# Preparing Strassen steps in an interleaved order, and 210 instead of 188 of them

## The chip, the core and the metric

The kernel runs on one NeuronCore of a Trainium2 chip. Times are device microseconds of that core. The weights are read from HBM in every run.

## What is computed

A decoder block for 256 tokens of 4096 channels in float32. Cut to what matters here:

```python
h = rmsnorm(x, norm_w)
proj = einsum('bsd,de->bse', h, w_in)            # 4096 x 20480
u_p, z_p, u_c, b_c, c_c, z_c, g_logit = split(proj)
y_pool = causal_multiscale_pool(u_p, pool_w, pool_scale) * silu(z_p)
y_conv = b_c * conv_b_w3(c_c * u_c) * silu(z_c)  # causal depthwise width 3
br = einsum('bsnc,ncd->bsnd', stack([y_pool, y_conv]), w_branch)   # 2 x 2048 x 4096
merged = sum(sigmoid(g_logit + gate_b) * br)
out = rmsnorm(x + einsum('bsd,de->bse', merged, w_out), final_norm_w)
```

Almost all of the arithmetic is in three products with large weights: `w_in`, `w_branch` and `w_out`.

## The kernel before

**Units and steps.** The work is cut into 32 units, each of which makes 256 tokens by 1024 output columns: twenty for `w_in` (named cu, cc, cz, cb for the convolution branch, pz, pu for the pooling branch, g for the gates, each with an index), eight for `w_branch` (b0_0 to b1_3) and four for `w_out` (o0 to o3). A unit of `w_in` or `w_out` has 16 steps, a unit of `w_branch` 8, so there are 448 steps on large weights. A step takes one 1 MB piece of weights (256 rows by 1024 columns), which SyncE loads into one of the `raw` buffers, and multiplies it with the 256 channels of activations that stand in `arena`.

**Precision.** Float32 is reached by splitting: ScalarE copies a value to the rounded type float32r (the high part, `act`), VectorE subtracts the high part from the value (the low part, `sub`). Each product is three matmuls: high by high, high by low, low by high. Split weights lie in `ring`, a circular store counted in blocks of 128 x 256 values; space is freed as TensorE's matmuls use it up.

**Two kinds of step.** A plain step ("P") has 8 products of 128 x 128 by 128 x 512, that is 24 matmuls; it splits its weights in two halves of 1024 columns per partition, one `act` and one `sub` each. A Strassen step ("S", the Winograd form) has 7 products, 21 matmuls, but adds weights before it splits them. Its VectorE instructions are, in this order: `V` (two sums at once, 1024 wide), the first half of `raw` overwritten with a sum (512), the low part of the three unsummed blocks (1536), another sum in `raw` (512), the low part of `V` (1024), the low part of the two sums in `raw` (1024). Ring space for it comes in pieces of 12, 8 and 8; a P step takes twice 8.

**Which steps are S.** For each unit a sequence of P and S is written out or spread by a formula. An operand in `arena` must be stored with its Strassen sums to serve an S step: 7 of the 16 channel pairs are stored so (`NS_X`), and 9 as P (`NP_X`). One of the P pairs, called `LATE`, has its sums computed and split separately and kept in other buffers (`late_sums`, `late_split`, `early_place`, `late_m`, the DRAM tile `late_d`), so that up to 8 steps of a unit can be S.

**The order of the work.** All instructions are emitted by one Python program that walks through the matmuls in TensorE's order; each engine then executes its own instructions in the order in which they were emitted. After each group of matmuls `after_group` calls `tick`, which takes one item from `queue` (the unit's epilogue, with `gap(n)` as pauses) and one piece of filling the next operands into `arena` (`pop_fill`), and then `pump`. `pump` emits the next pieces of preparation (`micros`) of the steps to come, up to `AHEAD` = 3 steps ahead, as far as the ring has room by then; it also issues the load into a `raw` buffer whose previous step is prepared. At the end of a unit the four shared banks with Strassen products are combined by `joins`, and the other banks are copied by ScalarE and added by `combine`.

VectorE's instructions of the preparation are all at line L72 (`tt`, through `add` and `sub`), ScalarE's at L69 (`act`), the matmuls of the steps at L1283 (`multiply`), loads by SyncE at L87, transfers by GpSimd at L91 and L94.

Of the kernel before, what the change touches and what calls it, by code (L numbers as in the profile page):

```python
# [26 lines left out]
F32 = mybir.dt.float32  # L27
# [5 lines left out]
P = 128  # L33
# [9 lines left out]
NP_X, NS_X = 9, 7  # L43
NB = 1
NP_Y, NS_Y = (6, 5), (2, 3)
RING = 60
NRAW = 3
# [9 lines left out]
def hybrid_block(ctx: ExitStack, tc: tile.TileContext, x, x_t, norm_t, w_first, w_in, pool_w, pool_scale,  # L57
# [70 lines left out]
    late_d = dram.tile([P, 5, P], F32, name="late_d")  # L128
# [62 lines left out]
    class Operand:  # L191


        def __init__(self, kind, view, region):
            self.kind, self.view, self.region = kind, view, region
            self.ready = False
            self.more = None
            self.more_ready = False

        def block(self, part, i):  # L200

            if self.kind == "S":
                return self.view[:, part, i]
            if i in self.more:
                return self.more[i][:, part]
            return self.view[:, part, {A12: 0, A22: 0, A11: 1, A21: 1}[i], i in (A22, A21)]
# [32 lines left out]

    rg = Ring(RING)  # L240

# [5 lines left out]
    class Step:  # L247
# [7 lines left out]
        def micros(self):  # L255
# [27 lines left out]
            if self.kind == "P":  # L283
                self.blocks, self.h, self.l = [None] * 2, [None] * 2, [None] * 2
                return self.pre + [(8, None, half(0)), (8, None, half(1))] + self.post
            if self.kind == "S":
                q = r.rearrange("p (i n) -> p i n", i=4)
                tv = V

                def sums(_):  # L290
                    add(tv, q[:, 0:1].to_broadcast([P, 2, NH]), q[:, 1:3])

                def direct(block):
                    self.bd = block
                    d = piece(block, 0, 12).rearrange("p (i a n) -> p i a n", i=3, a=2)
                    self.dh, self.dl = d[:, :, 0], d[:, :, 1]
                    act(self.dh, q[:, 1:4])
# [11 lines left out]
                def t24(block):  # L309
                    self.b24 = block  # L310
                    t = piece(block, 0, 8).rearrange("p (i a n) -> p i a n", i=2, a=2)
                    self.h24, self.l24 = t[:, :, 0], t[:, :, 1]
                    act(self.h24, q[:, 0:2])
                    sub(self.l24, q[:, 0:2], self.h24.bitcast(F32))

                return self.pre + self.post + [(0, None, sums), (12, None, direct), (8, None, t13), (8, None, t24)]
            if self.kind == "B":
                def parts(block):
# [4 lines left out]
                    sub(self.l, R, self.h.bitcast(F32))  # L323

                return [(16, lambda: self.unit.flags.get("base"), parts)]
            if self.kind == "M":
# [4 lines left out]
                def weights(block):  # L331
# [5 lines left out]
                    sub(self.l, q, self.h.bitcast(F32))  # L337

# [265 lines left out]
    LAST_FIRST = ('cc0',)  # L604
    SPREAD = {"cc1":(8,1),"cb1":(8,2),"cu1":{4,5,7,9,10,12,13,15},"cb0":(8,2),"cz0":(7,5),"pz0":{5,7,8,10,11,13,15},"pu0":(7,),"cz1":(7,5),"g1_3":(6,0),"pz1":(7,),"g0_0":(7,),"pu1":{4,6,8,10,12,13,15},"cc0":{2,4,6,8,10,13,15}}
# [26 lines left out]
    def in_unit(name, col, epi, seq=None, **kw):  # L632
        def src(i):
            return win[col // NU, i]
        if name in SPREAD:
            at = SPREAD[name]
            seq = at_places(at) if isinstance(at, set) else spread_sequence(*at)
# [5 lines left out]
        units.append(Unit(name, src, seq or seq_late, x_ops, epi, scaled=True, **kw))  # L643
# [3 lines left out]
    def conv_units(c, first=False):  # L647
# [32 lines left out]
        in_unit(f"cu{c}", base, lambda u: [], seq=seq_0 if first else spread_sequence(NS_X, 4), dst=Y)  # L680
        in_unit(f"cc{c}", base + 2 * HALF, c_epi, seq=seq_even if c else None)
        in_unit(f"cz{c}", base + 3 * HALF, z_epi)
        in_unit(f"cb{c}", base + HALF, b_epi, seq=seq_even)


    def pool_units(c):
# [5 lines left out]
        in_unit(f"pz{c}", HALF + c * NU, z_epi, seq=None if c else seq_turned)  # L692
# [4 lines left out]
    def make_bands(c):  # L697
        nonlocal sa, Y
        if c == 0:
            x_ops[LATE].more_ready = False  # L700

# [78 lines left out]
    def gate_unit(n, c, before=None):  # L780
# [7 lines left out]
        seq = {(0, 0): seq_late, (1, 3): spread_sequence(few)}.get((n, c), seq_even)  # L788
        if (n, c) in ((0,1),(1,1),(0,2),(1,2),(0,3),(1,0),):
            seq = spread_sequence(NS_X + 1, 1 if c else 2)  # L790
# [27 lines left out]

    def out_unit(c):
# [14 lines left out]
        seq = seq_even if c else seq_late  # L834
        if c in (2,):
            seq = spread_sequence(NS_X + 1)
        if c == 1:
            seq = at_places({2,4,6,7,9,11,13,15})

            late_s = [i for k, i in seq if k == 'S']  # L840
            late_s = iter(late_s[1:] + late_s[:1])
            seq = [(k, next(late_s) if k == 'S' else i) for k, i in seq]
        if c == 3:

            seq = spread_sequence(NS_X, 1, TAIL + 0)
        if c == 2:
            seq = at_places({2,4,6,7,9,11,13,15})
# [133 lines left out]
    def insert(u, c, owner):  # L981
# [6 lines left out]
        rest = psteps[5:]  # L988
        while ssteps:
            seq.append(ssteps.pop(0))  # L990
            if rest:
                seq.append(rest.pop(0))
        seq += rest
# [132 lines left out]
    LATE = NP_X - 1  # L1126

    def late_sums():
        o = x_ops[LATE]
        h, l = (o.view[:, part].bitcast(F32) for part in range(2))  # L1130
        q = sa[:, 4:8].rearrange("p (k t) c -> p k t c", t=2)
        add(q, h, l)
        q = q.rearrange("p k t c -> p k (t c)")
        mul(q, q, rbc[:, None].to_broadcast([P, 2, T]))
        sums_s(sa, [sa[:, i] for i in range(4, 8)])
        mul(sa[:, Q3], sa[:, Q3], std)
        move(late_d[:, 0:4], sa[:, 0:4])
        move(late_d[:, 4], sa[:, A11])

    def late_place(pool, o, blocks):  # L1140
        n = len(blocks)
        q = pool.tile([P, 2, n, P], F32R, name="sums")
        o.more = {b: q[:, :, i] for i, b in enumerate(blocks)}
        return q

    def late_split(o, place, src):

        q = []
        return [lambda: (q.append(place()), act(q[0][:, 0], src)),
                lambda: (sub(q[0][:, 1], src, q[0][:, 0].bitcast(F32)), setattr(o, "more_ready", True))]  # L1150

    early = []

    def early_place():

        pool = replace_by("early")
        src = pool.tile([P, 5, P], F32, name="early_src")
        move(src, late_d)
        early.extend(late_split(x_ops[LATE], lambda: late_place(pool, x_ops[LATE], (Q3, Q5, Q6, Q7, A11)), src))

    late = []

    def late_m():
        nonlocal Y
        pool = replace_by("late_m", lower)
        stages.pop()
        Y = pool.tile([P, 1, NU], F32, name="Y")
        sums_s(sa, [sa[:, i] for i in range(4, 8)])
        late.append(late_place(pool, m_ops[LATE], (Q3, Q5, Q6, Q7)))

# [12 lines left out]
    seconds = {14: 10, 15: 11, 16: 12, 17: 13, 19: 14, 21: 15, 28: 9}  # L1183
# [15 lines left out]
    before(23, late_sums)  # L1199
    before(40, early_place)  # L1200
    before(41, lambda: early[0]())
    before(42, lambda: early[1]())
# [30 lines left out]

    def pump():

        while True:
# [10 lines left out]
            if i < len(steps) and i <= state["limit"]:  # L1247
                s = steps[i]
                if s.src is None or s.raw is not None:
                    if state["micros"] is None:  # L1250
                        state["micros"] = deque(s.micros())
                    if state["micros"]:
                        size, guard, fn = state["micros"][0]
# [14 lines left out]
    for s in steps:  # L1268
        s.prepared = False
# [305 lines left out]
```

## Time and profile before

| | |
|---|---|
| median of three runs | 2378.24 us (2378.23 to 2379.2) |
| span of the profiled execution, first to last instruction | 2376.6 us |
| TensorE busy | 2364.3 us (99%), 10540 matmuls |
| VectorE busy | 2170.1 us (91%), 2195 instructions |
| ScalarE busy | 1392.8 us (59%) |
| GpSimd busy | 86.0 us (4%) |
| DMA | 551.25 MB, mean 232 GB/s |
| granted clock of TensorE | 0.999 |

The profile names a group of instructions by its line, engine and operation, then what it writes and reads (`ring<-raw`), the shape and the count; then busy time, mean duration, and the time that the engine idled before them with what ended the wait. The profile gives the profiled execution by its span only; the median of the runs is 1.6 us above that span.

### The profile page before, as it was taken

The numbers are of one execution on the slowest core, as the hardware profiler recorded it, in microseconds if no ns is written. First come the engines' busy times: TensorE is split into PE (matmuls) and PEld (weight loads), VectorE is DVE, ScalarE is ACT, GpSimd is POOL, SyncE is SP. The second block draws the span as 40 slices with busy tenths as digits, with TensorE's granted clock in tenths as the row PEclk, the third lists the DMA queues.
The fourth block names the chain that finished last, engine by engine and source line by source line (L and its number), as shares of the span: only waits on it lengthen the run. The fifth ranks groups of instructions, "written<-read, shape, count | busy, mean of one in ns | idle before, by whom it ended". The sixth has DMA issues, their size and how long they took to land.

```text
span 2376.6 us, 27878 instructions
## 1 busy us (share of the span) xinstructions
PE 2364.3 (99%) x10540; PEld 1957.5 (82%) x10540; DVE 2170.1 (91%) x2195; ACT 1392.8 (59%) x1452; POOL 86.0 (4%) x153
## 2 busy tenths in 40 slices
PE   9999999999999999999999999999999999999998
PEld 7888888888888888888888888888888888888886
DVE  8999999989989978979999999999898898799998
ACT  7565665656546555556655656556664556566554
POOL 0000000000010010000000000000100001000000
PEclk9999999999999999999999999999999999999999
DMA  8464665655665646655776667667766667567666
GB/s 337 161 238 170 235 251 211 217 211 213 212 239 217 238 183 221 231 200 201 259 247 214 235 237 235 228 238 260 263 249 230 226 250 289 209 214 265 241 240 264
DMA packets 83559, 551.25 MB, mean 232 GB/s; under 512 B 9616, under 2 KB 9872, under 8 KB 22240
## 3 DMA queue, kind: packets, MB, share of 16 engines
q1 hardware_dynamic: 68800, 484.51, 54.7%
q0 software_dynamic: 14192, 63.90, 9.6%
q8 instruction: 82, 1.34, 0.2%
q10 hardware_dynamic: 432, 1.07, 0.1%
q14 instruction: 53, 0.43, 0.1%
HBM read 516.60 MB, written 25.49 MB: 228 GB/s over the span
## 4 chain that ended last, share of the span: by engine, by line
PE 98%; DVE 1%; DMA 1%; ACT 0%; SPq 0%; issue 0%; DVEq 0%; ACTq 0%
PE sums L1283 74%; PE shared L1283 21%; PE shared L766 1%; PE shared L509 1%; DMA raw<-in_w_in_dram 0%; DVE R L72 0%; DVE ring L72 0%; DMA raw<-in_w_out_dram 0%; ACT ring L69 0%; PE shared L745 0%; SPq L87 0%; PE shared L746 0%; PE shared L748 0%; SPq L162 0%; ACT V L69 0%
## 5 line engine op out<-in xcount | busy, mean ns | idle before, releaser
L1283 PE MATMUL sums<-ring,arena 128*128 128x512 f32 x7890 | 1858.2, 390 | 0.5 <-ACT arena L69 0.4
L1283 PEld LDWEIGHTS sums<-ring,arena 128*128 128x128 f32 x7890 | 1478.3, 188 | 307.8 <-ACT ring L69 1.2
L69 ACT ACTIVATE ring<-raw 128x1024 fp32r<-128x1024 f32 (+2 forms) x902 | 997.5, 1145 | 703.9 <-DVE raw L72 297.3
L72 DVE TENSOR_TENSOR ring<-raw,ring 128x1024 fp32r<-128x1024 f32 (+2 forms) x902 | 1176.5, 1335 | 142.5 <-ACT ring L69 108.6
L1283 PE MATMUL shared<-ring,arena 128*128 128x512 f32 x2118 | 535.2, 389 | 0.0
L1283 PEld LDWEIGHTS shared<-ring,arena 128*128 128x128 f32 x2118 | 397.6, 188 | 82.5
L69 ACT ACTIVATE ring<-V 128x1024 fp32r<-128x1024 f32 x188 | 198.8, 1058 | 148.3 <-DVE V L72 112.7
L72 DVE TENSOR_TENSOR V<-raw 128x1024 f32<-128x1024 f32 x188 | 229.3, 1220 | 4.7 <-DMA raw<-in_w_in_dram 2.6
L72 DVE TENSOR_TENSOR ring<-V,ring 128x1024 fp32r<-128x1024 f32 x188 | 229.3, 1220 | 0.5 <-ACT ring L69 0.5
L72 DVE TENSOR_TENSOR raw<-raw 128x512 f32<-128x512 f32 x188 | 130.2, 693 | 6.5
L72 DVE TENSOR_TENSOR raw<-V,raw 128x512 f32<-128x512 f32 x188 | 130.0, 692 | 5.8
L72 DVE TENSOR_TENSOR R<-R,E 128x1024 f32<-128x1024 f32 (+1 forms) x49 | 77.5, 1591 | 1.6 <-ACT E L69 0.9
L72 DVE TENSOR_TENSOR R<-R,shared 128x512 f32<-128x512 f32 x87 | 59.5, 684 | 8.9 <-ACT R L69 5.0
L69 ACT ACTIVATE E<-sums,rin 128x512 f32<-128x512 f32 x76 | 50.0, 685 | 15.7 <-PE sums L1283 15.7
L69 ACT ACTIVATE arena<-sa 128x512 fp32r<-128x512 f32 (+2 forms) x42 | 22.4, 559 | 35.5 <-DVE sa L72 35.5
L1283 PE MATMUL shared<-ring,sums 128*128 128x512 f32 x138 | 35.9, 396 | 0.0
L1283 PEld LDWEIGHTS shared<-ring,sums 128*128 128x128 f32 x138 | 25.9, 188 | 6.0
L94 POOL DMA_DIRECT2D R<-E x8 | 7.2, 980 | 513.6 <-ACT ring L69 337.9
L69 ACT ACTIVATE E<-sums 128x512 f32<-128x512 f32 x40 | 22.2, 592 | 5.4 <-PE sums L1283 5.1
L72 DVE TENSOR_TENSOR arena<-sa,arena 128x512 fp32r<-128x512 f32 (+2 forms) x42 | 24.4, 606 | 0.7 <-ACT arena L69 0.7
L94 POOL DMA_DIRECT2D R<-in_gate_b_dram x9 | 10.1, 1119 | 356.0 <-DVE R L72 348.3
L509 PEld LDWEIGHTS shared<-ident,R 128*128 128x128 f32 x160 | 19.4, 140 | 4.2
(149 smaller groups left out, 515.8 us busy)
## 6 DMA issues: line engine op xcount, KB each, us to landing
raw<-in_w_in_dram SPq DMA_DIRECT2D x318, 1024.0 KB, 4.9
raw<-in_w_branch_dram SPq DMA_DIRECT2D x64, 1024.0 KB, 5.4
raw<-in_w_out_dram SPq DMA_DIRECT2D x64, 1024.0 KB, 5.0
gates_d<-R POOLq DMA_DIRECT2D x8, 1024.0 KB, 9.1
R<-in_gate_b_dram POOLq DMA_DIRECT2D x7, 1024.0 KB, 11.2
R<-E POOLq DMA_DIRECT2D x4, 1024.0 KB, 8.7
raw<-in_pool_w_dram SPq DMA_DIRECT2D x4, 1024.0 KB, 5.0
Y<-gates_d POOLq DMA_DIRECT2D x4, 1024.0 KB, 7.9
```

The lines of the kernel that those rows point to most:

```text
L69: return pin(nc.scalar.activation(dst, src, func, **kw))
L72: return pin(nc.vector.tensor_tensor(out=dst, in0=a, in1=b, op=op))
L94: return pin(nc.gpsimd.dma_start(dst, src, accum_op=ALU.add))
L509: pin(nc.tensor.transpose(shared(j)[:, i * T + t * P:i * T + (t + 1) * P], src[:, t, c:c + P], ident))
L766: pin(nc.tensor.matmul(o, a[:, k, ts], b[:, k], start=(k, i) == (0, 0), stop=(k, i) == (3, 2)))
L1283: pin(nc.tensor.matmul(ps, lhs, rhs, start=n == 0, stop=n == u.total[b] - 1))
```

## The change

- `NP_X, NS_X` goes from 9, 7 to 7, 9: nine channel pairs are stored with Strassen sums, two more than before, and the special `LATE` pair with all its code goes. `NB` (how many S slots of `arena` are two blocks longer) goes from 1 to 2, `RING` from 60 to 58 blocks, `NRAW` from 3 to 4 buffers. The space that software DMAs keep for descriptors is set to 2048 bytes of each partition.
- The P and S places of every unit are written out (`PLACES`, `GATE`, `OUT`). 210 of the 448 steps are S, before 188.
- The preparation of an S step is reordered and interleaved with its neighbours. ScalarE's copy of the three unsummed blocks comes first; then VectorE makes `V`, then the low part that the S step before still owes (`settle`), then the low part of the three blocks, then the first sum in `raw`; then the split of `V`, then the second sum. The low part of the two sums is put on `held` and emitted inside the next step's preparation. `head_of_next` emits the first ScalarE copy of the next step ahead of the last copy of this one. A P step's halves are split into a `high` and a `low` piece each.

The core of the diff:

```diff
-NP_X, NS_X = 9, 7
-NB = 1
+NP_X, NS_X = 7, 9
+NB = 2
-RING = 60
-NRAW = 3
+RING = 58
+NRAW = 4
...
+    held = []
+
+    def settle():
+
+        while held:
+            held.pop(0)()
...
+                def low(n):
+                    def f(_):
+                        sub(self.l[n], q[:, :, n * NH:(n + 1) * NH], self.h[n].bitcast(F32))
+                        settle()
+                    return f
+                return self.pre + [(8, None, high(0)), (0, None, low(0)), (8, None, high(1)), (0, None, low(1))] + self.post
...
-                def sums(_):
-                    add(tv, q[:, 0:1].to_broadcast([P, 2, NH]), q[:, 1:3])
                 def direct(block):
...
                     act(self.dh, q[:, 1:4])
+                def sums(_):
+                    add(tv, q[:, 0:1].to_broadcast([P, 2, NH]), q[:, 1:3])
+                    settle()
+                    sub(self.dl, q[:, 1:4], self.dh.bitcast(F32))
                     add(q[:, 0], tv[:, 0], q[:, 2])
-                    sub(self.dl, q[:, 1:4], self.dh.bitcast(F32))
-                    add(q[:, 1], q[:, 0], q[:, 3])
...
+                def t24(_):
+                    add(q[:, 1], q[:, 0], q[:, 3])
                     act(self.h24, q[:, 0:2])
-                    sub(self.l24, q[:, 0:2], self.h24.bitcast(F32))
-                return self.pre + self.post + [(0, None, sums), (12, None, direct), (8, None, t13), (8, None, t24)]
+                    def low24():
+                        sub(self.l24, q[:, 0:2], self.h24.bitcast(F32))
+                        self.prepared = True
+                    held.append(low24)
+                return self.pre + self.post + [(12, None, direct), (0, None, sums), (8, None, t13), (8, None, place24),
+                                               (0, lambda: head_of_next(self), t24)]
...
+        "cb0": (3, 5, 6, 8, 9, 11, 12, 14, 15),
...
+    GATE = (2, 4, 5, 7, 8, 10, 11, 13, 15)
...
+    OUT = ((5, 7, 8, 10, 11, 13, 15), (2, 4, 6, 7, 9, 11, 12, 13, 15), (2, 4, 6, 7, 9, 11, 13, 15),
+           (1, 3, 4, 6, 7, 9, 10, 12))
...
-    seconds = {14: 10, 15: 11, 16: 12, 17: 13, 19: 14, 21: 15, 28: 9}
+    seconds = {14: 10, 15: 11, 16: 12, 17: 13, 19: 14, 21: 15, 28: 9, 32: 8, 36: 7}
...
+    def head_of_next(s):
+
+        i = state["np"] + 1
+        if i == len(steps):
+            return True
+        t = steps[i]
+        if t.kind not in "PS" or t.pre or t.post and t.kind == "S" or t.started:
+            return True
+        if i <= state["limit"] and t.raw is not None:
+            t.started = micro(t)
+        return t.started or state["np"] <= state["now"] + 1
...
-    nc = _bacc.Bacc("TRN2", target_bir_lowering=False, num_devices=1)
+    nc = _bacc.Bacc("TRN2", target_bir_lowering=False, num_devices=1,
+                     dynamic_dma_scratch_size=2048)
```

More of the change, by code (lines that the diff above doesn't have):

```diff
@@ L1123, in x_parts @@
             sub(o.view[:, 1, a:b], sa[:, a:b], o.view[:, 0, a:b].bitcast(F32))
[L1126 to L1169, printed above, removed]
     def before(i, fn, *args):
@@ L1375, in hybrid_block @@
         for st in u.steps:
+            if not st.prepared:
+                settle()
             assert st.prepared, (u.name, st.kind)
@@ L1422, in hybrid_block @@
     for st in lead:
+        if not st.prepared:
+            settle()
         assert st.prepared, (last.name, st.kind)
```

120 lines of the change are left out of this document (51 added, 69 removed), and 12 rows, old and new, of the table PLACES.

## The prediction

> **What bounds the kernel now.** I read the page first, then the waits of every engine, then the timelines of TensorE and VectorE, then one unit alone.
>
> ```profile
> span 2376.6 us, 27878 instructions
> ...
> PE 2364.3 (99%) x10540; PEld 1957.5 (82%) x10540; DVE 2170.1 (91%) x2195; ACT 1392.8 (59%) x1452; POOL 86.0 (4%) x153
> ...
> PE 98%; DVE 1%; DMA 1%; ACT 0%; SPq 0%; issue 0%; DVEq 0%; ACTq 0%
> ```
>
> TensorE holds 98% of the chain that ended last. A busy TensorE can still be a stalled one, so the waits decide; these are all that the trace has for TensorE and its weight loads:
>
> ```profile
> PE shared L1034 <- DVE rout L1039: 1.1, 1, 1.1
> PE sums L1283 <- ACT arena L69: 0.4, 1, 0.4
> ...
> PEld sums L1283 <- ACT ring L69: 1.2, 2, 0.6
> PEld sums L1283 <- DVE ring L72: 0.5, 1, 0.5
> ```
>
> Three microseconds in all: in 2376.6 us TensorE never lacks operands. The time is then the number of matmuls by the interval of one. From TensorE's timeline in the middle of the run:
>
> ```profile
> 1002.00 1.52 PE L1283 MATMUL sums<-ring,arena 128*128 128x512 f32 x6
> 1003.36 2.20 PE L1283 MATMUL shared<-ring,arena 128*128 128x512 f32 x9
> 1005.40 0.84 PE L1283 MATMUL sums<-ring,arena 128*128 128x512 f32 x3
> ```
>
> From start to start, six take 1.36 us and nine take 2.04: 0.2267 us each. A P step (24) is 5.44 us, an S step (21) 4.76.
>
> The second-busiest engine is VectorE, at 91%, and an S step costs it much more than a P step. One unit of the gates, g0_1 (16 steps, 8 of them S; its first and last matmul counted off in the order of instructions), as a stretch of the windows and as VectorE's groups in it:
>
> ```profile
> 1200.70:1282.40 81.70, 81.70 (x361) 67.56 (x360) 75.73 (x71) 48.44 (x47) 1.80 (x2) 1.00 0.68 232
> ```
> ```profile
> L72 DVE TENSOR_TENSOR ring<-raw,ring 128x1024 fp32r<-128x1024 f32 x24 | 28.4, 1222 | 2.6 <-PE sums L1283 2.1
> L72 DVE TENSOR_TENSOR ring<-raw,ring 128x1536 fp32r<-128x1536 f32 x8 | 14.0, 1754 | 2.8 <-ACT ring L69 2.8
> L72 DVE TENSOR_TENSOR V<-raw 128x1024 f32<-128x1024 f32 x8 | 9.8, 1219 | 0.0
> L72 DVE TENSOR_TENSOR ring<-V,ring 128x1024 fp32r<-128x1024 f32 x8 | 9.7, 1218 | 0.0
> L72 DVE TENSOR_TENSOR raw<-raw 128x512 f32<-128x512 f32 x8 | 5.5, 692 | 0.3
> L72 DVE TENSOR_TENSOR raw<-V,raw 128x512 f32<-128x512 f32 x8 | 5.5, 692 | 0.3
> L72 DVE TENSOR_TENSOR R<-R,shared 128x512 f32<-128x512 f32 x4 | 2.7, 682 | 0.0
> L72 DVE TENSOR_TENSOR R<-R,E 128x1024 f32<-128x1024 f32 x2 | 2.4, 1218 | 0.0
> ```
>
> VectorE is busy 75.73 of 81.70 us, and ScalarE 48.44, so VectorE alone can become the next bound. What one instruction really takes is seen in its timeline:
>
> ```profile
> 1001.66 1.22 DVE L72 TENSOR_TENSOR ring<-V,ring 128x1024 fp32r<-128x1024 f32 x1
> 1002.95 3.50 DVE L72 TENSOR_TENSOR ring<-raw,ring 128x1024 fp32r<-128x1024 f32 x3
> 1006.36 1.22 DVE L72 TENSOR_TENSOR V<-raw 128x1024 f32<-128x1024 f32 x1
> 1007.62 0.69 DVE L72 TENSOR_TENSOR raw<-V,raw 128x512 f32<-128x512 f32 x1
> 1008.23 1.75 DVE L72 TENSOR_TENSOR ring<-raw,ring 128x1536 fp32r<-128x1536 f32 x1
> 1010.01 0.69 DVE L72 TENSOR_TENSOR raw<-raw 128x512 f32<-128x512 f32 x1
> 1010.62 1.22 DVE L72 TENSOR_TENSOR ring<-V,ring 128x1024 fp32r<-128x1024 f32 x1
> 1011.89 1.23 DVE L72 TENSOR_TENSOR ring<-raw,ring 128x1024 fp32r<-128x1024 f32 x1
> ```
>
> Three low parts that nothing holds up take 3.41 us (1002.95 to 1006.36), 1.14 each: one starts 0.08 before the last has ended. An instruction that depends on the one just ahead starts 0.03 to 0.04 after its end: `V` to the sum that reads it is 1.26, the 1536-wide low part to the sum that overwrites its source 1.78. So a held instruction costs 0.12 more. Free prices: 1.14 (1024 wide), 0.61 (512, from 1007.62 to 1008.23), 1.67 (1536, its 1.75 less 0.08). I use these below.
>
> **The matmuls.** 22 steps turn from 24 to 21 matmuls: 66 fewer, which the order of instructions confirms (10,536 matmuls in the program before, 10,470 after). No other matmul goes or comes. TensorE never waits now, so each is worth its interval: 66 x 0.2267 = 15.0 us. The floor is 2378.24 - 15.0 = 2363.3 (the profiled execution's span would be 2361.6, always 1.6 below). The order of matmuls at the end of the run, the start and the last three P steps keep their form; I give these ends plus or minus 1.
>
> **VectorE's work.** Free, an S step costs 3 x 1.14 + 2 x 0.61 + 1.67 = 6.3 us and a P step 2 x 1.14 = 2.3. Each conversion adds 4.0 us, 22 of them 88. The program has 2299 VectorE instructions instead of 2195: 88 are these, the other 16 are the sums and splits of two more pairs less those of `LATE`, some 4 us. Against that, the old order holds two instructions in each S step (the sum after `V`, the second sum after the 1536-wide low part), the new one none, since an older low part, or the low part of `V`, stands between: 188 x 2 x 0.12 = 45 us back. VectorE should show about 2230 us busy (94%).
>
> The mean is no bound; the unit is. g0_1 becomes 9 S and 7 P: 357 matmuls, 80.9 us. VectorE: 9 x 6.3 + 7 x 2.3 + four joins at 0.61 + two additions at 1.14 = 77.5 us in 74 instructions. That leaves 3.4 us in 81, where the old order has 8 x 6.54 + 8 x 2.3 + 4.7 = 75.4 of 81.6. I counted the 32 units the same way from the order of instructions; every one has less VectorE work than matmul time. Tightest are o0 (85.4 of 85.9) and o3 (59.9 of 60.5), then cb0 and cb1 (79.3 of 80.9). So VectorE keeps up on average, and a loss can only come where a unit bunches its work.
>
> **Where it bunches.** o0 also fills `arena` with operands from merged results, by instructions with these groups:
>
> ```profile
> L72 DVE TENSOR_TENSOR arena<-sa,arena 128x512 fp32r<-128x512 f32 x31 | 21.2, 685 | 0.7 <-ACT arena L69 0.7
> L72 DVE TENSOR_TENSOR arena<-Y,arena 128x256 fp32r<-128x256 f32 x4 | 1.7, 418 | 0.0
> L72 DVE TENSOR_TENSOR sa<-Y 128x128 f32<-128x128 f32 x12 | 3.4, 284 | 0.0
> ```
>
> Less 0.08 each, an operand's four sums are 0.8 us and its three low parts (512, 256, 128 wide) 1.14. In the new order the sixth to eleventh steps of o0 are S P S S P S: 4 x 4.76 + 2 x 5.44 = 29.9 us of matmuls. What is emitted beside them for VectorE: 5 `V`, 4 low parts of `V`, 4 held low parts and 4 halves of P steps (17 at 1.14), 5 wide low parts (1.67), 9 sums in `raw` (0.61), 3 sets of operand sums and 4 of operand low parts: 19.4 + 8.35 + 5.5 + 2.4 + 4.6 = 40.2 us. The last 4.6 of it (a half, `V`, a wide low part, a sum) are for later steps. The rest, 35.6, ends with the held low part of the twelfth step (S), whose first product with it is the sixth, 15 matmuls or 3.4 us into that step: needed at 29.9 + 3.4 = 33.3. It is 2.3 us late, and TensorE waits. The same count in o3 gives 0.5 late twice, elsewhere nothing over the deadline. I add 2.3 + 1.0 = 3.3.
>
> From below, 0: VectorE may begin a piece before TensorE reaches the step beside which it is emitted. From above: preparation runs mostly two steps ahead of TensorE in the new order, where the old one is two or three ahead about equally often (counted at the step starts), and VectorE waits on ScalarE's copies now as follows:
>
> ```profile
> ACT ring L69 <- PE sums L1283: 208.0, 153, 4.8
> ...
> DVE ring L72 <- ACT ring L69: 114.7, 112, 4.5
> ```
>
> The copies themselves wait for TensorE to free the ring, so most of the 114.7 is VectorE having caught up. If a tenth of it were real lateness and came on top, 11 us. So 0 to 14, and 3.3 as worked out.
>
> **The rest, at nothing.**
>
> ```profile
> L69 ACT ACTIVATE ring<-raw 128x1024 fp32r<-128x1024 f32 x706 | 712.7, 1054 | 463.3 <-DVE raw L72 297.3 <-PE sums L1283 113.3 <-DMA raw<-in_w_in_dram 17.3
> ...
> L69 ACT ACTIVATE ring<-raw 128x1536 fp32r<-128x1536 f32 x188 | 279.2, 1485 | 238.5 <-issue 141.1 <-PE sums L1283 67.9 <-DMA raw<-in_w_in_dram 7.6
> ```
>
> ScalarE gains 22 x 1.5 us (one 1536-wide and two 1024-wide copies in place of two 1024-wide) and stays near 60% of the span. Loads: the same 476 transfers of SyncE, each now issued when the step four back is prepared, and "prepared" comes later by the held piece; they land in 4.9 us, one step's time, with two steps to spare. The smaller space for descriptors concerns GpSimd's transfers:
>
> ```profile
> q0 software_dynamic: 14192, 63.90, 9.6%
> ...
> raw<-in_w_in_dram SPq DMA_DIRECT2D x318, 1024.0 KB, 4.9
> ...
> R<-in_gate_b_dram POOLq DMA_DIRECT2D x7, 1024.0 KB, 11.2
> ```
>
> The slowest land after 11.2 us; the epilogue leaves 12 ticks of 6 matmuls, 16.3 us, before the result is used. Five transfers of `LATE` go, no other is added, so 5 us of cover stand, and GpSimd is 4% busy.
>
> Sum: 2378.24 - 15.0 + 3.3 = 2366.6 us.
>
> **Rivals.** *VectorE becomes the bound* (slower). Its place is every unit with nine S steps: 3.4 us of slack are gone when 29 of the 74 instructions (40%) are held 0.12 us each, because ScalarE's part comes just too late. From there each further tenth of held instructions costs a nine-S unit about 0.9 us. At 60%, eleven such 16-step units lose 1.8 us each (20), o0 and o3 7 and 3, the others some 7: 2363.3 + 37 = 2400. For it: each S step has three hand-overs from ScalarE, which itself waits in order for TensorE. Against: the new order puts one to three VectorE instructions between a copy and its use. 6%.
>
> *Nothing overlaps* (slower). If every instruction began only 0.035 after the end of the one ahead, a unit like g0_1 would need 77.5 + 74 x 0.12 = 86.4 us against 80.9, and with the others summed likewise about 114 us would be lost: 2477. The three low parts in 3.41 us, and 0.61 for a sum of 0.69, speak against it: 1%. The Trainium skill, in "VectorE: DVE Perf Modes", section "The DRAIN you can't avoid", says that the next instruction does not start until the pipe has emptied and that leaving out semaphores does not help; by that rule the reordering frees nothing and this rival holds, and the trace disagrees by the 0.08 us of overlap.
>
> *The lead is too short* (no change). At each unit's end the joins, the additions and the next S step fall together while ScalarE waits for the last banks. If that costs 0.8 us in each of the 15 units with nine S steps or tight ones, with the 3.3 above it is 15: 2378. 8%.
>
> *The descriptor space is too small* (slower). If each of the seven 1 MB additions of the gate bias waited for an earlier transfer to land, 10 us later against 5 of cover, the loss is 35: 2394 to 2398. Against it: 14,192 packets over some hundred transfers and 16 engines is about nine for each. 2%.
>
> **How the numbers follow.** The forecast, with stalls of 0 to 10 us, has 83%. A measurement of this kernel can tell about 0.2%, 4.8 us, from no change: faster means below 2373.5, and forecast stalls above 10 fall to "same". Faster 0.83, same 0.08, slower 0.09. The range goes from the floor less 1 at the ends, 2362, to 14 us of stalls, 2377, which takes in most of the third rival.
>
> **What would show it.** Right: 10,470 matmuls, a span near 2365, VectorE near 2230 us busy, and under TensorE's waits a few microseconds on `ring`, most near the twelfth step of o0. The low part after `V` should start before `V` ends. Wrong: TensorE waiting for VectorE or ScalarE in many units, windows of gate units longer than 81 us, VectorE near 97% (second rival near 100%), or landings of GpSimd's transfers far above 11 us.

## The result, and the profile after

The changed kernel takes 2557.11 us (median of four runs, 2554.57 to 2558.63), the kernel before in the same session 2378.72 us: 1.0749 times as long, interval 1.0734 to 1.0764. The forecast was 2366.6, with a range up to 2377. The page of the profiled execution, its first lines and the engines' shares of the chain that ended last:

```profile
span 2554.4 us, 27577 instructions
...
PE 2419.2 (95%) x10474; PEld 1970.0 (77%) x10474; DVE 2236.4 (88%) x2299; ACT 1416.5 (55%) x1477; POOL 85.6 (3%) x148
...
PE 74%; DVE 12%; issue 8%; ACT 5%; DMA 0%; ACTq 0%; DVEq 0%; SPq 0%
```

TensorE has 66 matmuls fewer, as worked out, and yet its busy time rose from 2364.3 to 2419.2. VectorE is busy 2236.4 us, close to the 2230 that was worked out, but its share *fell* from 91% to 88%: it isn't overloaded, it waits. TensorE idles 2554.4 - 2419.2 = 135.2 us, before 12.3. The waits say for whom (line, engine and tile that waited, the releaser; us in total, times, longest):

```profile
PEld shared L1279 <- DVE ring L72: 111.8, 66, 3.4
PE shared L1279 <- DVE ring L72: 85.5, 57, 2.9
...
PE sums L1279 <- DVE ring L72: 23.0, 11, 2.8
...
PE sums L1279 <- ACT ring L69: 13.0, 8, 2.1
```

Of TensorE's idle time 108.5 us are waits for VectorE's low parts in `ring`, 13.0 for ScalarE's high parts. One step further back, the two preparing engines wait for each other:

```profile
ACT ring L69 <- DVE raw L72: 506.8, 185, 6.6
...
DVE ring L72 <- ACT ring L69: 269.3, 207, 4.0
```

VectorE's wait for ScalarE was 114.7 us in 112 times before. It is 269.3 in 207 now, close to one for each of the 210 S steps.

Where it happens: stretches of the windows (length; busy time of each engine with its instructions; granted clock; DMA share and GB/s). The first is unit cb0, the second g0_1, the fourth o0, each from its first matmul to that of the next unit; the third lies in the units of `w_branch`.

```profile
core 0: us, PE busy (x) PEld busy (x) DVE busy (x) ACT busy (x) POOL busy (x), PEclk, DMA share, GB/s
265.97:359.81 93.84, 84.30 (x358) 68.13 (x357) 79.83 (x75) 52.25 (x51) 1.58 (x2) 0.96 0.55 199
1312.04:1402.53 90.49, 85.06 (x359) 69.07 (x357) 78.60 (x74) 50.01 (x48) 1.79 (x2) 0.96 0.60 217
2000.00:2100.00 100.00, 100.00 (x451) 82.93 (x450) 85.64 (x81) 57.73 (x67) 4.19 (x7) 1.00 0.62 231
2181.81:2276.54 94.73, 88.70 (x380) 71.64 (x379) 82.46 (x105) 52.68 (x65) 2.14 (x4) 0.96 0.48 178
```

The prediction put g0_1's 357 matmuls at 80.9 us and VectorE's 74 instructions in it at 77.5. The count is right and VectorE's 78.60 nearly so, but the unit lasts 90.49. cb0 loses 12.9 us and o0 8.8 (its matmuls were put at 85.9); in the units of `w_branch` TensorE hardly stops. The loss is spread over the units with many S steps.

Counting the matmuls step by step in the trace places it more closely. TensorE has 59 stalls of more than 0.6 us in the units of `w_in` and `w_out`, and 58 of them stand in an S step that directly follows another S step, as 71 of the 210 S steps do. Eight units end with two S steps (places 14 and 15), and each loses 2.8 to 4.9 us there, some 35 us together; in cb0, about ten matmuls before its end:

```profile
352.16 0.50 PE L1279 MATMUL sums<-ring,arena 128*128 128x512 f32 x1 [1.64 <-ACT ring L69]
355.50 1.22 PE L1279 MATMUL sums<-ring,arena 128*128 128x512 f32 x2 [2.84 <-DVE ring L72]
```

One such loss, read in the timeline of the changed kernel (start, us, engine, line, operation, tiles, shapes, number of instructions; in brackets the idle time before and its releaser). The three lines at the top show the same place three steps earlier, with a short stall; from 1446.42 on an S step is being finished and a P step follows:

```profile
1431.31 2.36 DVE L72 TENSOR_TENSOR ring<-raw,ring 128x1024 fp32r<-128x1024 f32 x2 [2.16 <-ACT ring L69]
...
1433.72 0.73 PE L1279 MATMUL shared<-ring,arena 128*128 128x512 f32 x2 [0.66 <-DVE ring L72]
...
1434.29 6.30 PE L1279 MATMUL sums<-ring,arena 128*128 128x512 f32 x27
...
1446.42 0.68 DVE L72 TENSOR_TENSOR raw<-raw 128x512 f32<-128x512 f32 x1
...
1447.22 4.33 ACT L69 ACTIVATE ring<-raw 128x1024 fp32r<-128x1024 f32 x4 [3.30 <-DVE raw L72]
1447.23 1.75 PE L1279 MATMUL shared<-ring,arena 128*128 128x512 f32 x7
1449.26 3.50 DVE L72 TENSOR_TENSOR ring<-raw,ring 128x1024 fp32r<-128x1024 f32 x3 [2.15 <-ACT ring L69]
...
1451.67 1.03 PE L1279 MATMUL shared<-ring,arena 128*128 128x512 f32 x2 [2.70 <-DVE ring L72]
...
1452.50 7.63 PE L1279 MATMUL sums<-ring,arena 128*128 128x512 f32 x27
```

At 1446.42 VectorE makes the second sum of the S step. ScalarE has stood idle 3.30 us for it, because the copy of the two sums is next in its queue. VectorE's next instruction in turn is the low part of the P step's first half. Its copy stands behind the copy of the sums, so VectorE waits for *two* copies, 2.15 us. Only then comes the held low part of the S step, the second of the three, done at about 1451.62 (two low parts take 2.36 us in this timeline, three 3.50), and TensorE has needed it since 1448.97: it stands 2.70 us. Three steps earlier VectorE waited just as long (2.16 us), and TensorE stood only 0.66: the wait costs what the preparation isn't ahead by. Afterwards 27 matmuls take 7.63 us instead of the 6.30 at the top: part of the stall is paid a second time, since the clock falls (last section).

The transfers were no part of it. GpSimd's slowest, the gate bias, lands after 9.7 us (11.2 before). SyncE's loads of weights land later (5.5 us, 4.9 before), but ScalarE waits for those of `w_in` only 2.0 us in all (24.9 before):

```profile
q0 software_dynamic: 13840, 62.66, 9.0%
...
raw<-in_w_in_dram SPq DMA_DIRECT2D x318, 1024.0 KB, 5.5
...
R<-in_gate_b_dram POOLq DMA_DIRECT2D x7, 1024.0 KB, 9.7
```

**What the order of instructions shows.** `head_of_next` is to emit the next step's first copy ahead of the copy of the sums; then the wait just shown would not occur. Its last line lets it give up when the step being prepared (`np`) is no further than the one next to be multiplied (`now` + 1):

```python
        if i <= state["limit"] and t.raw is not None:
            t.started = micro(t)
        return t.started or state["np"] <= state["now"] + 1
```

`micro(t)` needs ring space for the first piece (8 blocks for a P step, 12 for an S step). Two S steps fill 56 of the 58 blocks. Counted in the program as emitted, the copy went ahead in only 94 of the 210 S steps; in 116 it gave up. ScalarE's copies in the trace, in order of time, bear this out: in 93 S steps a copy of the next step stands ahead of the copy of the sums.

**Theory.** Where it gives up, the queues of ScalarE and VectorE cross as in the timeline; the second sum, made directly ahead of its copy, sets how long. **Rivals.** VectorE's load for 210 S steps is too much in any order; the ring of 58, the raw buffers or the descriptor space; the places of the S steps.

### The profile page after: what moved, and what is told of

Its sections match the earlier page's. It is cut to its first block, busy times and chain, and to the rows that moved or that the text cites. A ratio compares the mean times of both kernels' runs of the same rounds, so it can differ in the third digit from the quotient of the medians.

```text
span 2554.4 us, 27577 instructions
## 1 busy us (share of the span) xinstructions
PE 2419.2 (95%) x10474; PEld 1970.0 (77%) x10474; DVE 2236.4 (88%) x2299; ACT 1416.5 (55%) x1477; POOL 85.6 (3%) x148
## 4 chain that ended last, share of the span: by engine, by line
PE 74%; DVE 12%; issue 8%; ACT 5%; DMA 0%; ACTq 0%; DVEq 0%; SPq 0%
PE sums L1279 57%; PE shared L1279 15%; DVE ring L72 7%; ACT ring L69 4%; DVE raw L72 3%; DVE V L72 1%; PE shared L804 1%; PE shared L535 1%; DVE R L72 0%; DVE arena L72 0%; ACT E L69 0%; DMA raw<-in_w_first_dram 0%; ACTq L69 0%; ACT R L69 0%; ACT arena L69 0%
## 5 line engine op out<-in xcount | busy, mean ns | idle before, releaser
L1279 PE MATMUL sums<-ring,arena 128*128 128x512 f32 x7596 | 1832.7, 395 | 36.3 <-DVE ring L72 23.0
L1279 PEld LDWEIGHTS sums<-ring,arena 128*128 128x128 f32 x7596 | 1442.7, 191 | 349.4 <-DVE ring L72 28.2
L72 DVE TENSOR_TENSOR ring<-raw,ring 128x1024 fp32r<-128x1024 f32 (+2 forms) x902 | 1190.7, 1348 | 275.4 <-ACT ring L69 263.3
L1279 PE MATMUL shared<-ring,arena 128*128 128x512 f32 x2520 | 669.6, 400 | 86.5 <-DVE ring L72 85.5
L1279 PEld LDWEIGHTS shared<-ring,arena 128*128 128x128 f32 x2520 | 478.2, 192 | 213.2 <-DVE ring L72 111.8
L69 ACT ACTIVATE ring<-V 128x1024 fp32r<-128x1024 f32 x210 | 221.9, 1057 | 235.7 <-DVE V L72 205.8
L72 DVE TENSOR_TENSOR ring<-V,ring 128x1024 fp32r<-128x1024 f32 x210 | 256.3, 1220 | 0.4 <-ACT ring L69 0.4
L72 DVE TENSOR_TENSOR V<-raw 128x1024 f32<-128x1024 f32 x210 | 256.0, 1219 | 0.0
L535 PE MATMUL shared<-ident,R 128*128 128x128 f32 x160 | 22.6, 272 | 0.0
L804 PE MATMUL shared<-ring 128*128 128x512 f32 x96 | 22.1, 389 | 0.0
```

Source lines behind the costliest of these rows:

```text
L69: return pin(nc.scalar.activation(dst, src, func, **kw))
L72: return pin(nc.vector.tensor_tensor(out=dst, in0=a, in1=b, op=op))
L535: pin(nc.tensor.transpose(shared(j)[:, i * T + t * P:i * T + (t + 1) * P], src[:, t, c:c + P], ident))
L804: pin(nc.tensor.matmul(o, a[:, k, ts], b[:, k], start=(k, i) == (0, 0), stop=(k, i) == (3, 2)))
L1279: pin(nc.tensor.matmul(ps, lhs, rhs, start=n == 0, stop=n == u.total[b] - 1))
```

## Experiments

The kernel before measured 2378.3 to 2378.5 us beside each of them. "Floor" is the time with every matmul at its interval and no wait: 2363.3 us for 210 S steps, and 0.68 us (three matmuls) more for each step fewer.

**1. A larger ring, three raw buffers** (the store for the fourth pays for it).

```diff
-RING = 58
-NRAW = 4
+RING = 66
+NRAW = 3
```

> The changed kernel with a ring of 66 blocks and three raw buffers in place of 58 and four (the same memory). Theory A (round trip): when the second weight sum of an S step is emitted, the next step's first ScalarE copy should already stand in ScalarE's queue; in the changed kernel the ring has no room for it in 116 of 210 S steps, so VectorE waits some 2.3 us for two copies made one after the other. With 66 blocks the order of instructions has 22 such steps left, so the waits of VectorE for ScalarE on the ring fall from 269 us to about 50 to 100, and the time to 2365 to 2400 us. Theory B (capacity: 210 S steps bunch more VectorE work than TensorE's time covers, whatever the ring): still above 2500.

Measured: 2467.63 us, ratio 1.0378 (1.0361 to 1.0396). That lies between the two forecasts. The copy is given up in 22 steps instead of 116, and 89 us come back; VectorE's waits fall less than expected. The waits have new names in them:

```profile
ACT ring L69 <- DMA raw<-in_w_in_dram: 179.7, 102, 6.6
...
DVE ring L72 <- ACT ring L69: 155.3, 119, 6.1
...
DVE V L72 <- DMA raw<-in_w_in_dram: 26.1, 13, 3.6
```

In the new order a raw buffer is released only by the held low part, so three buffers are too few and the loads come late. The run changes two things in opposite directions; it speaks for the theory but does not isolate it.

**2. The old order inside the changed kernel.** Places, sizes and the 210 steps stay.

```diff
-                return self.pre + self.post + [(12, None, direct), (0, None, sums), (8, None, t13), (8, None, place24),
-                                               (0, lambda: head_of_next(self), t24)]
+                return self.pre + self.post + [(0, None, sums), (12, None, direct), (8, None, t13), (8, None, t24)]
...
-                return self.pre + [(8, None, high(0)), (0, None, low(0)), (8, None, high(1)), (0, None, low(1))] + self.post
+                return self.pre + [(8, None, half(0)), (8, None, half(1))] + self.post
```

> The changed kernel (210 S steps, its places, ring of 58 blocks, four raw buffers, 2048 bytes of descriptors) with the old order of preparation inside a step: nothing held over, no interleaving, halves of P steps whole. Theory A: the long waits go, since both sums are made ahead of the wide low part and ScalarE's copies come early; VectorE pays 0.12 us twice per S step, 50 us in all: 2365 to 2410 us. Theory B: above 2500. Theory C (a ring of 58 blocks and a lead of one or two steps is too short for any order): above 2450.

Measured: 2426.92 us, ratio 1.0208 (1.0193 to 1.0223), above the range of theory A and below those of B and C.

```profile
PE 2369.6 (98%) x10474; PEld 1942.9 (80%) x10474; DVE 2264.7 (93%) x2299; ACT 1418.2 (59%) x1477; POOL 86.0 (4%) x148
```
```profile
DVE ring L72 <- ACT ring L69: 98.4, 86, 3.4
PEld shared L1253 <- DVE ring L72: 33.2, 34, 3.0
```

With the same places and sizes, the order alone is 130 us of the loss. VectorE is 28.3 us less busy in the new order (2264.7 to 2236.4), and waits 171 us longer for ScalarE (98.4 to 269.3). But the old order with 210 steps is 64 us over the floor too, so there are two causes.

**3. The new order with 192 steps**, at places like those before.

```diff
-        "cb0": (3, 5, 6, 8, 9, 11, 12, 14, 15),
+        "cb0": (2, 4, 6, 7, 9, 10, 12, 14),
...
```

> The changed kernel with 192 S steps instead of 210: the places of the units of the first product as before, those of the last product as changed; new order, ring of 58. In the order of instructions 64 S steps (before 116) find no room for the next step's first copy. Theory A: the loss scales with these steps: floor 2363.3 + 18 x 0.68 = 2375.5, plus 64/116 of the 194 us lost, about 2480 us. Theory B: no loss at 192, 2375 to 2390.

Measured: 2456.12 us, ratio 1.0327 (1.0312 to 1.0342), 24 us less than theory A expected; VectorE busy 2162.7 us, less than in the kernel before, and its waits for ScalarE still 235.8 us in 191 times. 81 us over its floor of 2375.5: the new order loses where VectorE's load is no greater than before.

**4. The sizes alone**, in the kernel before.

```diff
-RING = 60
-NRAW = 3
+RING = 58
+NRAW = 4
...
+                     dynamic_dma_scratch_size=2048)
```

> The kernel before with the three sizes of the change alone: ring of 58, four raw buffers, 2048 bytes of descriptors; old order, 188 S steps. Theory A: 2376 to 2390, the sizes hurt only through the new order. Theory C: above 2430, the lead falls to one or two steps here too (at the step starts 13 times one, 372 times two, 66 times three, before 3, 243 and 205).

Measured: 2381.99 us (ten runs), ratio 1.0015 (1.0005 to 1.0024). Ring, raw buffers and descriptor space together cost 3.5 us here, so the sizes are not a cause of their own; the ring of 58 still matters where the order or the 210 steps need room (1 and 6). VectorE waits 142.5 us for ScalarE in this run, against 114.7 before, and TensorE hardly notices: such a wait is harmless as long as the preparation is ahead.

**5. The second sum made early**, right after the first, two instructions and a split before its copy.

```diff
                     add(q[:, 0], tv[:, 0], q[:, 2])
+                    add(q[:, 1], q[:, 0], q[:, 3])
...
                 def t24(_):
-                    add(q[:, 1], q[:, 0], q[:, 3])
                     act(self.h24, q[:, 0:2])
```

> The changed kernel with one instruction moved: the second weight sum of an S step stands right after the first, ahead of the split of V, so ScalarE's copy of the two sums no longer follows the end of the step's VectorE work. Ring 58, four raw buffers, 210 steps. Theory A (the round trip second sum, ScalarE's copy, the next step's copy, VectorE again is what costs): VectorE's waits for ScalarE on the ring fall from 269 us to about 100 and the time to 2400 to 2440, near the old order's 2427, with 25 us of VectorE added by the dependent pair. Theory B (VectorE's capacity and the short lead alone): stays within 1% of 2557.

Measured: 2469.8 us, ratio 1.0387 (1.0368 to 1.0405): 87 us come back from moving one line. That is 30 us above theory A's range, and the waits are 175 us where about 100 were expected.

```profile
ACT ring L69 <- DVE raw L72: 305.6, 164, 3.3
...
DVE ring L72 <- ACT ring L69: 175.4, 159, 3.8
```

ScalarE's wait for `raw` fell by 201 us, VectorE's for ScalarE by 94. 43 us to the old order remain.

**6. The old order with more lead:** the edit of 2 with `RING = 66`, `NRAW = 3`.

> The old order of preparation with 210 S steps, a ring of 66 blocks and three raw buffers. The old order frees a raw buffer with its step and lost 64 us above the floor with a ring of 58, where the preparation was at most two steps ahead 388 times of 451; here 254. If the short lead is what it lost by: 2365 to 2400. If VectorE has too little time in the nine-S units whatever the lead: 2415 to 2435, as with 58.

Measured: 2407.98 us, ratio 1.0125 (1.0109 to 1.0141), between the two forecasts. Lead gives back 19 of the 64 us; 45 stay over the floor with VectorE busy 2263.1 of 2405.4 us (94%).

**7. Less work for VectorE:** the edit of 2, and one line fewer.

```diff
-                    add(q[:, 1], q[:, 0], q[:, 3])
```

> The old order with 210 S steps, ring 58, four raw buffers, and the second weight sum of each S step left out (the operand of one of its seven products is not summed): 210 instructions of 0.61 to 0.72 us less on VectorE, everything else as in the old-order run of 2427. If VectorE's load is the bound there: TensorE's waits go and the time is the floor, 2363 to 2370, which also measures what 66 matmuls are worth. If the lead is the bound: above 2400.

Measured: 2366.79 us, ratio 0.9951 (0.9933 to 0.9968). Its page, its waits and the unit g0_1:

```profile
PE 2350.0 (99%) x10474; PEld 1945.8 (82%) x10474; DVE 2112.7 (89%) x2089; ACT 1433.8 (61%) x1477; POOL 87.1 (4%) x148
```
```profile
DVE ring L72 <- ACT ring L69: 201.7, 163, 3.8
...
PEld shared L1252 <- DVE ring L72: 3.5, 2, 1.9
```
```profile
1190.88:1271.80 80.92, 80.92 (x358) 67.00 (x357) 73.19 (x65) 50.08 (x48) 1.79 (x2) 1.00 0.67 234
```

3.5 us over the floor: the term for the matmuls was right, and 80.9 us for g0_1 to the digit. With 152 us less work, VectorE can wait 201.7 us for ScalarE and TensorE doesn't see it. The run takes away a hand-over too (the copy no longer waits for this sum), so it shows that instruction and its wait to be the old order's 64 us, not how they divide.

**8 and 9. New and old order at 190 steps**, with room for both: eight pairs with sums, a ring of 63, four raw buffers, at most 8 S steps in a unit. The second also has the edit of 2.

```diff
-NP_X, NS_X = 7, 9
-NB = 2
-RING = 58
+NP_X, NS_X = 8, 8
+NB = 1
+RING = 63
...
-    GATE = (2, 4, 5, 7, 8, 10, 11, 13, 15)
+    GATE = (1, 3, 5, 7, 8, 10, 12, 14)
```

> The new order of preparation where neither VectorE's load nor the ring should bind: 190 S steps (at most eight in a unit, eight channel pairs stored with sums), ring of 63, four raw buffers. Floor 2378.24 - 2 x 0.68 = 2376.9. In the order of instructions 38 of 190 S steps find no room for the next step's first copy. Theory A (the new order loses by its hand-overs between VectorE and ScalarE wherever that copy is not ahead): 2420 to 2450. Theory B (the load of nine-S units): 2376 to 2385.

> The same 190 steps, places, ring of 63 and four raw buffers with the old order of preparation. Both theories: 2376 to 2384. Its difference to the run before it is the order alone.

Measured: new order 2418.34 us, ratio 1.0171 (1.0157 to 1.0185); old order 2386.11, ratio 1.0032 (1.002 to 1.0045). Both lie some 2 us outside their ranges (below 2420 and above 2384). Nothing differs but the order, and it costs 32 us. VectorE's waits for ScalarE, in the new order and in the old:

```profile
DVE ring L72 <- ACT ring L69: 194.1, 155, 3.7
...
DVE ring L72 <- ACT ring L69: 106.8, 105, 4.5
```

The copy is given up in 38 of the 190 steps of the new order.

**10. A search for something better: old order, 196 steps, ring of 71,** three raw buffers, the `LATE` pair gone.

```diff
-NP_X, NS_X = 9, 7
+NP_X, NS_X = 8, 8
...
-RING = 60
+RING = 71
```

> An attempt to beat the kernel before: old order, eight channel pairs with sums, 196 S steps with at most eight in a unit, the freed descriptor space given to the ring (71 blocks, three raw buffers). Floor 2378.24 - 8 x 0.68 = 2372.8. If units of eight S steps fit VectorE as they do in the kernel before: 2372.5 to 2376. If the extra steps in the units of the pooling and z branches do not fit: 2378 to 2390.

Measured: 2383.26 us, ratio 1.0022 (1.0013 to 1.0031). Not faster; 10.5 us over its floor of 2372.8.

**11. Old order, 206 steps, ring of 66, and additions in GpSimd's transfers** instead of on VectorE, as two units had them already:

```diff
-            elif u.name in ['g0_0', 'o0']:
+            elif u.halves and u.added is not None and u.name != 'o2':
```

> Old order, ring of 66, three raw buffers, 206 S steps (cu1, cz1, pz0 and o3 one fewer each), and in the gate units and o1 the two additions of the last partial results (2.3 us of VectorE per unit) made by GpSimd's accumulating transfers. Floor 2366. If VectorE's load in the nine-S units is what lost 44 us in the old order with a ring of 66, then taking 2.3 of 80 us from nine of them recovers most of their 0.4 to 2.1 us each and the four steps another 5: 2378 to 2395. If not the load: about 2405.

Measured: 2394.06 us, ratio 1.006 (1.0044 to 1.0075), 28 us over its floor of 2366.0. VectorE is busy 2228.8 us instead of 2263.1 in experiment 6, and 17 us of that run's 45 are gone. The run also has four S steps fewer, and the two changes are not separated.

**12. No look-ahead at all** in the changed kernel:

```diff
-                                               (0, lambda: head_of_next(self), t24)]
+                                               (0, None, t24)]
```

> The changed kernel (210 Strassen steps, ring of 58 KB, new order) in which no step ever starts the next step's first copy ahead of its own copy of the two sums: the condition of the last piece is dropped. In the changed kernel that copy went ahead in 94 of 210 steps. Theory (ScalarE's queue holds the copy of the sums, which waits for VectorE, in front of the next step's copy, so VectorE waits for two copies one after the other): the 116 steps in which the changed kernel gave up are all that it loses over its own order at work, so the loss of about 194 us over the matmul floor of 2363 grows with the count, to 194 x 210 / 116 = 351 at most; the early steps of a unit have slack, so 2620 to 2715, with VectorE's waits for ScalarE up from 269 us to 350 or more. Rival (giving up costs little, the late second sum is the whole of it): within 20 us of 2557 and waits near 269.

Measured: 2665.16 us, ratio 1.1206 (1.1187 to 1.1224).

```profile
DVE ring L72 <- ACT ring L69: 372.6, 246, 4.0
...
PEld shared L1279 <- DVE ring L72: 157.3, 92, 4.3
PE shared L1279 <- DVE ring L72: 120.3, 82, 3.9
```

94 more steps give up, and it is 108 us longer: 1.15 us for each. Ring, buffers and the sum's place in VectorE's order stay. Nothing waits for room any more, so the sum and its copy are emitted sooner if anything; the giving up is shown to cost time.

**13. The early sum at 190 steps:** the edit of 5 in kernel 8.

> New order, 190 Strassen steps, ring of 63 KB, four raw buffers, and the second weight sum made right after the first instead of just ahead of its copy. With the late sum this was 2418.3, with the old order 2386.1. Theory (a late sum and a look-ahead that gives up share the loss; at 63 KB it gives up in 38 of 190 steps): the late sum is about two thirds, as it was at 210 steps (87 of 130), so 2418 - 21 = 2397, between 2392 and 2403. Rival 1 (the late sum is all of it): 2386 or below. Rival 2 (the look-ahead's gaps are all of it): 2415 or above.

Measured: 2392.66 us, ratio 1.0061 (1.0046 to 1.0076).

```profile
ACT ring L69 <- DVE V L72: 166.9, 92, 5.8
DVE ring L72 <- ACT ring L69: 157.9, 146, 3.7
ACT ring L69 <- DVE raw L72: 135.7, 121, 3.1
```

ScalarE's wait for `raw` was 370.2 us in kernel 8. 25.7 of the 32.2 us are gone, 6.6 to the old order remain.

## Why the prediction was wrong, by its own steps

The 194 us over the floor divide so by the runs: 64 with 210 S steps in the old order (2), 130 by the new order, of which 87 return when one sum moves up (5) and 43 remain. The look-ahead's price is not a further share to be added, since both act on the same wait: the copy of the sums holds up the next step's copy for as long as it waits for the sum, and then for its own 1.05 us. How far the two overlap is argued, not measured: no run has the early sum without the look-ahead.

- **Matmuls, right.** 66 fewer, 15.0 us; without VectorE's excess the kernel runs at 2366.79 (7).
- **VectorE's prices, right as a load.** 2236.4 us busy against 2230. But the prediction's own terms, 2170.1 + 88 + 4 - 45, give 2217 and not its 2230: of the 0.12 us for a held instruction only the 0.08 of lost overlap is busy time, and 188 x 2 x 0.08 = 30 gives 2232. For 210 steps that is 34 us; the order's difference was measured at 28.3 (2264.7 to 2236.4).
- **The place of the second sum, put at nothing, wrong.** The prediction counted the new place, behind the split of `V`, only as a gain for VectorE, and nothing for ScalarE, whose copy waits for this sum. Moved up, the sum returns 87 of the 130 us that the order costs (5), and 25.7 of 32.2 at 190 steps (13).
- **The walk through o0, wrong.** It summed VectorE's instructions between two deadlines as if each found its high part copied. A utilisation of 99% was allowed to fit. No unit was checked for the time of a hand-over there and back, and that is where all nine-S units lost, 4.5 us or more each: g0_1 with 77.5 us of work in 80.9 took 90.49. The 2.3 us in o0 was the right kind of sum without the term that mattered, 2.15 us of waiting in one S step.
- **The look-ahead, wrong.** "The new order puts one to three VectorE instructions between a copy and its use" was read from the diff. In the emitted order it holds for 94 steps of 210. The order of instructions was there to be counted, and was used for matmuls and VectorE's work only, not for ScalarE's queue against VectorE's. Giving up in the other 94 steps as well costs 108 us more (12).
- **The lead, misread.** "Two steps ahead" at the step starts means that the step being multiplied and the next are prepared, no more. At 58 blocks that is all the ring can hold of S steps.
- **"If a tenth of it were real lateness", wrong as a bound.** The reading of the 114.7 us was not the fault: experiments 4 and 7 have 142.5 and 201.7 with TensorE undisturbed. The fault was to bound the changed kernel's lateness by a wait that the change itself redraws; it went to 269.3.
- **The first rival** named the kind and the place: VectorE in every unit with nine S steps, ScalarE's part just too late. It was priced with 0.12 us for a held instruction, where the waiting instruction loses 2.15, and so had 2400 and 6%. Its sign, "VectorE near 97%", points the wrong way: an engine that bounds by waiting shows a lower share.
- **The other rivals.** The sizes, put at nothing, cost 3.5 us (4). With them alone the gate bias lands after 12.1 us (11.2 before), so the descriptor space was not it. "Nothing overlaps" is out: three low parts still take 3.50 us. The section that the prediction quotes there, "The DRAIN you can't avoid" in "VectorE: DVE Perf Modes" of the Trainium skill, itself adds that a next operation which is not held starts earlier, so the overlap does not contradict it. "The lead is too short" was partly right in its place: some 35 us of stalls stand near the ends of eight units, 2.8 to 4.9 us each where it reckoned with 0.8. The others stand inside the units.
- **Where it bunches, misjudged.** The walk found lateness in o0 and o3 only. The stalls stand in almost every unit, where two S steps are neighbours. No run spreads the same 210 steps otherwise, so what the neighbourhood itself costs is not shown.
- **Left out: the clock.** TensorE should have been busy 2364.3 - 15.0 = 2349.3 us and was 2419.2. The clock explains some 47 of these 70 us, about a quarter of the loss: so much the trace's clock records give when laid over TensorE's busy time (93.7 us of it at half the clock). The mean clock, 0.977 against 0.999 before, bounds it at 56. Most of the rest is counting: a matmul's record lasts 0.39 us and the next starts after 0.2267, so each of some 90 pauses adds at least 0.16 us to the busy time.

What stays open: how the 43 us left after the early sum divide between the copies still given up and the other hand-overs, and how the old order's 64 divide between load and waiting. No version with all its sums beat the kernel before. Its 188 steps leave VectorE 206 us idle; the old order with 190, 196, 206 and 210 steps (9, 10, 11, 6) leaves 209, 182, 164 and 142 us, and loses 9, 10, 28 and 45 us over the floor. Their rings differ too (63, 71, 66 and 66 blocks), so this is no curve of VectorE's load alone.

## What to carry to other kernels

Where two engines hand work to and fro within each step, don't compare the sum of one engine's instructions with the time available: walk both queues together, in the order as emitted, and add for each hand-over what stands ahead of it in the other queue. A look-ahead that may give up must be counted in the built program, at the buffer sizes it gets; and an operation that another engine's queue waits for belongs as early as its inputs allow, ahead of work that is only local. Where other engines wait for an engine whose busy share falls, as here, the fall is a sign of lock-step, not of slack.

## What the runs showed of the hardware

A stall of TensorE can be paid a second time. Behind the 2.70 us stall of the timeline, the granted clock in short windows of the changed kernel:

```profile
1436.00:1447.20 11.20, 11.20 (x51) 9.28 (x50) 10.88 (x11) 4.45 (x4) 0.00 (x0) 1.00 0.86 345
1451.67:1452.67 1.00, 0.99 (x3) 0.79 (x4) 1.00 (x1) 0.00 (x0) 0.00 (x0) 0.63 0.23 25
1452.67:1453.67 1.00, 1.00 (x4) 0.81 (x3) 1.00 (x2) 0.00 (x0) 0.00 (x0) 0.50 0.57 115
1453.67:1454.67 1.00, 1.00 (x4) 0.71 (x4) 1.00 (x2) 0.69 (x1) 0.00 (x0) 0.50 0.94 393
1454.67:1456.00 1.33, 1.33 (x6) 1.11 (x5) 1.33 (x2) 0.37 (x1) 0.00 (x0) 0.75 1.06 444
1456.00:1459.70 3.70, 3.70 (x18) 3.07 (x17) 3.63 (x5) 1.69 (x2) 0.00 (x0) 1.00 0.64 266
```

1.00 ahead of it and again from 1456, and 0.50 between: by the shares of the windows (0.74 of the first, two whole ones, half of the fourth) for about 3.4 us. Eight matmuls in a row start 0.427 us apart there instead of 0.2267. That is 1.33 us more in the 27 matmuls and 0.30 in the two ahead of them, for a stall of 2.70; the stall of 0.66 cost nothing behind it. The Trainium skill, in "TensorE: Matmul & The Clock Gate", section "Part 1: The HAM clock gate", knows a full and a half clock, gives 426.7 ns for a matmul of 512 columns at the half one, and has the full clock return after about 3.4 us of work; the trace agrees with all three. The Trainium skill has the clock fall there after an idle window of about 3.4 us; here 2.70 us between two matmuls were enough.

The length of a stall alone does not decide it in this run. One of 1.90 us was followed by the half clock and one of 2.70 us was not:

```profile
1068.79 0.73 PE L1279 MATMUL shared<-ring,arena 128*128 128x512 f32 x2 [1.90 <-DVE ring L72]
...
1716.30 0.74 PE L1279 MATMUL shared<-ring,arena 128*128 128x512 f32 x2 [2.70 <-DVE ring L72]
```
```profile
1069.63:1073.04 3.41, 3.41 (x10) 2.63 (x9) 3.41 (x4) 1.06 (x1) 0.00 (x0) 0.50 0.93 327
...
1716.30:1719.70 3.40, 3.40 (x15) 2.78 (x16) 3.40 (x3) 1.06 (x1) 0.00 (x0) 1.00 0.63 210
```
